# A decoder block's attention: the softmax sums' reciprocals reach all partitions through DRAM instead of through TensorE transposes

## The chip, the cores and the metric

The kernel runs on one core of one Trainium2 chip. The metric is the device time of one execution in microseconds (us), lower is better. The kernel before takes 2318.57 us, the median of three runs (2317.03 to 2318.62). The profile shown here is of one further execution of it.

An engine is one of the core's processors, each with its own in-order instruction stream: PE (TensorE, matrix multiplications), DVE (VectorE), ACT (ScalarE), POOL (GpSimd) and SP (SyncE, which here issues nearly all the DMA transfers). An instruction that waits for another engine or for a transfer holds up everything behind it on its own engine.

## What is computed

The block adds attention and a gated recurrence to a residual stream. The change touches the attention alone:

```
def forgetting_attention(q, k, v, f_logit):
    ...
    def one_block(args):
        qi, ci, bi = args
        qpos = bi * Q_BLOCK + jnp.arange(Q_BLOCK)
        s = jnp.einsum('bhqd,bhkd->bhqk', qi, k, preferred_element_type=jnp.float32) * scale
        s = s + (ci[:, :, :, None] - c[:, :, None, :])
        s = jnp.where(kpos[None, :] <= qpos[:, None], s, -jnp.inf)
        w = jax.nn.softmax(s, axis=-1)
        return jnp.einsum('bhqk,bhkd->bhqd', w.astype(v.dtype), v)
```

There are 8 heads of width 128 and a sequence of 2048 positions. All is float32.

## The kernel before, in words

Every large product is made of three matrix multiplications (`mm3`, lines 60 to 62): an operand is split into a high part, rounded to the format that TensorE takes, and the low rest, and high by high, high by low and low by high are added up in PSUM, the accumulation memory.

The program has three stages. The first (to about 1140 us) makes q, k, v and the gates and runs the recurrence. The second, the attention, follows until about 1740 us. The third mixes the two branches and applies the last gate.

The attention works in **units**: a unit is a head h and a block g of 512 query positions (g from 0 to 3, so 32 units, numbered n). A unit needs keys and values only up to its own end, so block g has 4g+4 key blocks of 128. The schedule is written out by hand in **slots**; each key block of each unit has one slot, and `t0[n]` is the slot at which unit n's probabilities begin to be used. `run_slot(t)` emits, in this order:

- `before[t]`: the loads that were put into this slot (SP)
- the score pieces of a coming unit (`score_units`): `mm3` into a PSUM tile `sbank`, then on DVE (L629) the bias is added, the running row minimum kept in `m` and the result written to `pr`
- `add_values` for the key block of three slots ago (`AHEAD` = 3): `mm3` of values and turned probabilities into `obank`. There is **one** `obank` buffer, so a unit's first `add_values`, in slot t0+3, needs the former unit's result to have been read out
- when that was a unit's last key block, which is in slot t0+2 of the next unit: `finish_unit`, on DVE (L690), `on` = `obank` times `rb`. It reads `obank` out, and the buffer is free
- `turn_probs`: four PE transposes of the probabilities `pr` into a PSUM tile `tbank` (L665), then the split into `th` on ACT (L46) and `tl` on DVE (L52)
- `spread_sums`, in a unit's second slot (t0+1)
- `gate_unit` (L693) and the exponentials of rows that are complete (ACT, L638), which also give the row sums into `r4`
- one slot ahead of t0: the reciprocals of the sums, in place (L842)

The reciprocals stand in `r4` as four columns, one number for each query on its partition. `rb` must hold, on every partition, the 512 numbers along the row. `spread_sums` makes it with four PE transposes of a broadcast column (L684) and an ACT copy out of PSUM (L686):

```
b = psT.tile([P, 512], F32, name="tbank")
for i in range(4):
    nc.tensor.transpose(b[:, i * P:(i + 1) * P], u.r4[:, i:i + 1].broadcast_to([P, P]), ident)
u.rb = av.tile([P, 512], F32, name="rb")
nc.scalar.activation(u.rb, b, AF.Copy)
```

SP issues in this stage the queries `qf`, keys and values `kvf` of the next head, the biases `bias` and `dg`, the gates `gs`, and the stores of `ya_d` (L710), which wait for `gate_unit`. SP is not tied to slots: it runs ahead until an instruction of its queue has to wait. In the last head it also loads the output weights (`kvf` from `in_w_o_dram`), and in the last unit the recurrent branch (`yf`, L716), which ACT and POOL split into `yh` and `yo`; the product of these with the weights is worked off between the last unit's slots (`fill`).

Of the kernel before, what the change touches and what calls it, by code (L numbers as in the profile page):

```python
# [8 lines left out]
F32 = mybir.dt.float32  # L9
# [6 lines left out]
P = 128  # L16
# [49 lines left out]
def hymba_kernel(ctx: ExitStack, tc: tile.TileContext, x, xT, pT, w_t, w_v3, w_v4, w_o, w_ple, w_pg,  # L66
                 w_gates, vecs, rows, mgrp, out):
    nc = tc.nc
# [12 lines left out]
    r_d = dram.tile([NH * 4, 512], F32, name="r_d")  # L81
# [57 lines left out]
    def pool_(stack, name, bufs=1, side="left", space=None):  # L139
        kw = {"side": side} if space is None else {"side": side, "space": space}  # L140
        return stack.enter_context(tc.tile_pool(name=name, bufs=bufs, reuse_waits="tile", **kw))
# [317 lines left out]
    def load_piece(h, n):  # L459
        c = n // 2  # L460
        f = ap.tile([P, 4, P], F32, name="kvf", bufs=3)
        if n % 2 == 0:
            nc.sync.dma_start(out=f.rearrange("p a b -> p (a b)"), in_=kT_d[h, :, c * 512:(c + 1) * 512])
        else:
            nc.sync.dma_start(out=f, in_=v_d[h, :, c * 4:c * 4 + 4])
        pieces[h, n] = f

    def split_piece(h, n):
        if n == 0:
            s = Ctx()  # L470
            kv = kvB if h % 2 else kvA
            s.kh = kv.tile([P, S], F32R, name="kh")
            s.kl = kv.tile([P, S], F32R, name="kl")
            s.vh = kv.tile([P, TB, P], F32R, name="vh")
            s.vl = kv.tile([P, TB, P], F32R, name="vl")
            heads[h] = s
        s = heads[h]
        f = pieces.pop((h, n))
        c = n // 2
        if n % 2 == 0:  # L480
            cs = slice(c * 512, (c + 1) * 512)
            split(nc, f.rearrange("p a b -> p (a b)"), s.kh[:, cs], s.kl[:, cs], "act", "pool")
        else:
            bs = slice(c * 4, c * 4 + 4)
            split(nc, f, s.vh[:, bs], s.vl[:, bs], "act", "pool")
# [119 lines left out]
    av = pool_(p2, "av", 2)  # L605
# [54 lines left out]
    def turn_probs(g, u, sb):  # L660

        q0 = max(0, sb - 4 * g)
        b = psT.tile([P, 512], F32, name="tbank")
        for i in range(q0, 4):
            nc.tensor.transpose(b[:, i * P:(i + 1) * P], u.P[i][:, sb * P:(sb + 1) * P], ident)  # L665
        th = av.tile([P, 512], F32R, name="th", bufs=THB)
        tl = av.tile([P, 512], F32R, name="tl", bufs=THB)
        n = slice(q0 * P, 512)
        split(nc, b[:, n], th[:, n], tl[:, n], "act", "dve")
        u.parts[sb] = (th, tl, n)  # L670

    def add_values(h, g, u, sb):
        s = heads[h]
        nsb = 4 * g + 4
        if sb == 0:
            u.o = psO.tile([P, 512], F32, name="obank")
        th, tl, n = u.parts.pop(sb)
        mm3(nc, u.o[:, n], (s.vh[:, sb], s.vl[:, sb]), (th[:, n], tl[:, n]), sb == 0, sb == nsb - 1)

    def spread_sums(u):  # L680
# [7 lines that stand above are left out]
    def finish_unit(h, g, u):  # L688
        u.on = av.tile([P, 512], F32, name="on")
        nc.vector.tensor_tensor(out=u.on, in0=u.o, in1=u.rb, op=ALU.mult)  # L690

    def gate_unit(u):
        nc.vector.tensor_tensor(out=u.gs, in0=u.on, in1=u.gs, op=ALU.mult)  # L693

    def add_squares(h, g, u):
        on = u.on
        cs = slice(g * 512, (g + 1) * 512)
        eng = nc.vector if (h, g) == (NH - 1, 3) else nc.gpsimd
        if h == 0:
            nc.gpsimd.tensor_tensor(out=acca[:, cs], in0=on, in1=on, op=ALU.mult)  # L700
        else:
            eng.tensor_tensor(out=on, in0=on, in1=on, op=ALU.mult)
            eng.tensor_tensor(out=acca[:, cs], in0=acca[:, cs], in1=on, op=ALU.add)

    def load_gate(h, g, u):
        u.gs = av.tile([P, 512], F32, name="gs")
        nc.sync.dma_start(out=u.gs, in_=gT_d[h, :, g * 512:(g + 1) * 512])

    def store_y(h, g, u):
        nc.sync.dma_start(out=ya_d[h, :, g * 512:(g + 1) * 512], in_=u.gs)  # L710
# [22 lines left out]
    stages = [(h, g) for h in range(NH) for g in range(4)]  # L733
    NS = len(stages)
    t0, t = [], 8
# [4 lines left out]
    units = {0: u0}  # L740
    before = {}
    after = {}

    def at(d, slot, f):
        d.setdefault(max(slot, 0), []).append(f)
# [11 lines left out]
    def begin_unit(n):  # L757
        h, g = stages[n]
        u = units[n]
        u.parts = {}  # L760
        u.units = score_units(h, g, u)
# [16 lines left out]
        at(after, min(lo + 4, s0 - 1) if n > 1 else 0, lambda n=n: mask_u(units[n]))  # L778
    for n, (h, g) in enumerate(stages):
        at(before, max(t0[n] - 4, t0[n - 1] + 7) if n else t0[n] + 1, lambda h=h, g=g, n=n: load_gate(h, g, units[n]))  # L780
    for h in range(1, NH):
        base = t0[4 * (h - 1)]
        for p_ in range(8):
            a = base + (13 if p_ == 0 else 17 + 3 * p_)
            at(before, a - 6, lambda h=h, p_=p_: load_piece(h, p_))
            at(after, a, lambda h=h, p_=p_: split_piece(h, p_))
# [21 lines left out]
    def run_slot(t, fill=None):  # L808
        for f in before.pop(t, ()):
            f()  # L810
        post = []
        for n, j in s_at.pop(t, ()):
            if j == 0:
                begin_unit(n)
            f, a, z = units[n].units[j]
            e = f(a, z)
            if e is not None:
                post.append(e)
        if fill is not None:
            fill()  # L820
        done = None
        if t - AHEAD in slots:
            n, sb = slots[t - AHEAD]
            h, g = stages[n]
            add_values(h, g, units[n], sb)
            if sb == 4 * g + 3:
                done = units.pop(n)
                finish_unit(h, g, done)
                at(after, t + 3, lambda: add_squares(h, g, done))
                at(before, t + 4, lambda: store_y(h, g, done))  # L830
        if t in slots:
            n, sb = slots[t]
            turn_probs(stages[n][1], units[n], sb)
            if sb == 1:
                spread_sums(units[n])
        if done is not None:
            gate_unit(done)
        for e in post:
            e()
        if t + 1 in t0[:NS]:  # L840
            r4 = units[t0.index(t + 1)].r4
            nc.vector.reciprocal(r4, r4)  # L842
        for f in after.pop(t, ()):
            f()

    for t in range(last_t0 + 1):
        run_slot(t)
# [42 lines left out]
    def fill():  # L890
        tb, k = todo.pop(0)
        recurrent_half(tb, (k,))
        if k == KD - 1:
            store_m(tb, av, "th")
            if filling[0]:
                at(before, filling[0] + 1, lambda: load_yf(yl_d, tb + 2))
                at(after, filling[0] + 4, lambda: split_yf(tb + 2))
            else:
                next_y(tb)
# [3 lines left out]
    for t in range(last_t0 + 1, end):  # L903
        filling[0] = t
        run_slot(t, fill if last_t0 + 6 <= t < t0[NS] + AHEAD else None)
    filling[0] = 0
    for t in sorted(set(before) | set(after)):
        run_slot(t)
# [214 lines left out]
```

## Time and profile before

| | us |
|---|---|
| median of three runs | 2318.57 |
| the profiled execution, whole | 2320.89 |
| its span in the trace | 2319.0 |
| of it 0 to 1140 (first stage): PE busy | 1133.00 |
| of it 1140 to 1740 (attention): PE busy | 565.37 |
| of it 1740 to 2319 (third stage): PE busy | 569.72 |

The 1.9 us between the span and the whole execution lie around the program. In rows of the trace a name such as `obank<-th,vh` is the tile written and the tiles read; `x4` counts merged instructions; in the timeline the first number is the start and the second the duration, both in us, and a bracket behind a row is the time that its engine was idle before it, with what came last. PE's matrix multiplications overlap, so on PE the distance between starts is what one costs, not its duration.

### The profile page before, as it was taken

What the parts mean: (1) busy time and instruction counts of PE and PEld (TensorE: products, weight loads), DVE (VectorE), ACT (ScalarE), POOL (GpSimd) and SP (SyncE); (2) the same over time, 40 slices, a digit from 0 to 9 for tenths busy, and PEclk for the clock granted to TensorE, in tenths of its full rate; (3) what the DMA queues carried; (4) which work ended last, traced back from release to release, by engine and by line L of the source; (5) the groups of instructions that cost most, each with busy time, mean ns of one, the idle gap of its engine ahead of it and who ended that gap; (6) DMA issues with size and microseconds to landing.
All of it is one profiled execution on the core that took longest, in us unless ns stands there. A gap on an engine that the chain in (4) does not pass through costs nothing.

```text
span 2319.0 us, 30716 instructions
## 1 busy us (share of the span) xinstructions
PE 2268.1 (98%) x11425; PEld 1887.5 (81%) x11425; DVE 1207.6 (52%) x2190; ACT 926.2 (40%) x1558; POOL 676.7 (29%) x597
## 2 busy tenths in 40 slices
PE   8999999999999999999899999999999999999999
PEld 8998888888888888888777888888877887888887
DVE  5222675454545454646478878788823213333333
ACT  7311433333333232323366666766734323211111
POOL 0120322322323232323033434343444223222221
PEclk9999999999999999999999999999999999999999
DMA  9411112121212121212444454444446435433332
GB/s 337 137 51 37 53 55 71 45 76 37 84 37 84 37 85 37 82 37 78 147 133 130 149 153 143 137 133 128 147 122 199 152 129 191 125 109 118 108 107 77
DMA packets 169013, 249.02 MB, mean 107 GB/s; under 512 B 14240, under 2 KB 87200, under 8 KB 168864
## 3 DMA queue, kind: packets, MB, share of 16 engines
q1 hardware_dynamic: 168720, 247.03, 33.6%
q8 instruction: 89, 1.46, 0.3%
q14 instruction: 60, 0.49, 0.1%
q10 hardware_dynamic: 144, 0.05, 0.0%
HBM read 171.26 MB, written 75.76 MB: 107 GB/s over the span
## 4 chain that ended last, share of the span: by engine, by line
PE 89%; DVE 4%; DMA 2%; ACT 2%; issue 2%; POOL 1%; SPq 1%; DVEq 0%; ACTq 0%; POOLq 0%
PE bank L60 23%; PE bank L62 23%; PE bank L61 23%; PE tbank L665 4%; PE obank L60 2%; PE obank L61 2%; PE obank L62 2%; DVE pr L629 2%; PE sbank L60 2%; PE sbank L61 2%; PE sbank L62 2%; DMA kvf<-in_w_o_dram 1%; PE bank L1023 1%; ACT pr L638 1%; DVE tl L52 1%
## 5 line engine op out<-in xcount | busy, mean ns | idle before, releaser
L60 PE MATMUL bank<-xh,wh 128*128 128x512 f32 x1280 | 506.0, 395 | 0.0
L61 PE MATMUL bank<-xl,wh 128*128 128x512 f32 x1280 | 505.9, 395 | 0.0
L62 PE MATMUL bank<-xh,wl 128*128 128x512 f32 x1280 | 505.9, 395 | 0.0
L61 PEld LDWEIGHTS bank<-xl,wh 128*128 128x128 f32 x1280 | 240.5, 188 | 58.1
L62 PEld LDWEIGHTS bank<-xh,wl 128*128 128x128 f32 x1280 | 240.5, 188 | 58.0
L60 PEld LDWEIGHTS bank<-xh,wh 128*128 128x128 f32 x1280 | 240.5, 188 | 57.7
L52 DVE TENSOR_TENSOR tl<-tbank,th 128x512 fp32r<-128x512 f32 (+1 forms) x320 | 193.4, 608 | 93.4 <-ACT th L46 88.6
L46 ACT ACTIVATE th<-tbank 128x512 fp32r<-128x512 f32 (+1 forms) x320 | 168.5, 529 | 139.9 <-PE tbank L665 133.0
L52 POOL TENSOR_TENSOR wl<-wf,wh 128x512 fp32r<-128x512 f32 x70 | 96.0, 1392 | 265.0 <-ACT wh L46 265.0
L638 ACT ACTIVATE pr<-pr,m 128x128 f32<-128x128 f32 (+15 forms) x128 | 154.0, 1203 | 47.7 <-DVE m L629 47.0
L665 PE MATMUL tbank<-ident,pr 128*128 128x128 f32 x1088 | 172.0, 273 | 0.5 <-DVE tl L52 0.5
L665 PEld LDWEIGHTS tbank<-ident,pr 128*128 128x128 f32 x1088 | 134.1, 140 | 29.7 <-DVE tl L52 0.7
L52 POOL TENSOR_TENSOR yo<-yf,yh 128x1024 fp32r<-128x1024 f32 x32 | 76.8, 2400 | 258.2 <-ACT yh L46 251.8
L60 PE MATMUL bank<-wvh,xh 128*128 128x256 f32 (+1 forms) x512 | 144.2, 286 | 7.0 <-ACT wvh L46 7.0
L60 PE MATMUL obank<-th,vh 128*128 128x512 f32 (+1 forms) x320 | 124.7, 390 | 22.4 <-ACT th L46 11.6
L62 PE MATMUL bank<-wvh,xl 128*128 128x256 f32 (+1 forms) x512 | 144.6, 284 | 0.0
L61 PE MATMUL bank<-wvl,xh 128*128 128x256 f32 (+1 forms) x512 | 144.4, 284 | 0.0
L60 PE MATMUL sbank<-kh,qh 128*128 128x512 f32 (+3 forms) x320 | 134.9, 422 | 7.5 <-DVE m L629 6.5
L61 PE MATMUL obank<-tl,vh 128*128 128x512 f32 (+1 forms) x320 | 117.7, 368 | 1.2 <-DVE tl L52 0.6
L62 PE MATMUL obank<-th,vl 128*128 128x512 f32 (+1 forms) x320 | 117.5, 367 | 0.0
L61 PE MATMUL sbank<-kl,qh 128*128 128x512 f32 (+3 forms) x320 | 116.5, 364 | 0.0
L62 PE MATMUL sbank<-kh,ql 128*128 128x512 f32 (+3 forms) x320 | 116.1, 363 | 0.0
(218 smaller groups left out, 4599.4 us busy)
## 6 DMA issues: line engine op xcount, KB each, us to landing
wf<-in_w_t_dram SPq DMA_DIRECT2D x80, 256.0 KB, 3.0
xr<-in_x_dram SPq DMA_DIRECT2D x16, 512.0 KB, 6.7
v_d<-vo SPq DMA_DIRECT2D x64, 128.0 KB, 2.1
kT_d<-st SPq DMA_DIRECT2D x32, 256.0 KB, 2.1
yl_d<-G SPq DMA_DIRECT2D x32, 256.0 KB, 2.1
qT_d<-st SPq DMA_DIRECT2D x32, 256.0 KB, 2.1
gT_d<-st SPq DMA_DIRECT2D x32, 256.0 KB, 2.1
dg<-nb_d SPq DMA_DIRECT2D x32, 256.0 KB, 7.5
```

Of the source, the lines that this page charges most:

```text
L46: nc.scalar.activation(hi, src, AF.Copy)
L52: eng.tensor_tensor(out=lo, in0=src, in1=f32(hi), op=ALU.subtract)
L60: nc.tensor.matmul(out, lhsT=wh, rhs=xh, start=start, stop=False)
L61: nc.tensor.matmul(out, lhsT=wh, rhs=xl, start=False, stop=False)
L62: nc.tensor.matmul(out, lhsT=wl, rhs=xh, start=False, stop=stop)
L629: nc.vector.tensor_tensor_reduce(out=pr[0][:, a:z], in0=b[:, :z - a], in1=u.dg[i][1] if z == L else u.bias[:, a:z], scale=-1.0, scalar=BIG ...
L638: nc.scalar.activation(pr[0][:, :L], pr[0][:, :L], AF.Exp, bias=m2, scale=-1.0, accum_out=u.r4[:, i:i + 1])
L665: nc.tensor.transpose(b[:, i * P:(i + 1) * P], u.P[i][:, sb * P:(sb + 1) * P], ident)
L1023: nc.tensor.transpose(b[:, k * P:(k + 1) * P], ht[:, kk * P:(kk + 1) * P], ident)
```

## The change

For the units with g > 0 (24 of 32) the reciprocals are no longer turned on TensorE. `store_sums` writes the 128x4 tile to a row of 512 floats in DRAM (`r_d`), in slot t0+1; `load_sums` reads that row back into all 128 partitions, in slot t0+4. Both are issued by SP. The units with g = 0 keep `spread_sums`.

```
+    def store_sums(n):
+        nc.sync.dma_start(out=r_d[n].rearrange("(q p) -> p q", p=P), in_=units[n].r4)
+
+    def load_sums(n):
+        units[n].rb = av.tile([P, 512], F32, name="rb")
+        nc.sync.dma_start(out=units[n].rb, in_=r_d[n:n + 1, :].broadcast_to([P, 512]))
...
+    for n, (h, g) in enumerate(stages):
+        if g > 0:
+            at(before, t0[n] + 1, lambda n=n: store_sums(n))
+            at(before, t0[n] + 4, lambda n=n: load_sums(n))
...
-            if sb == 1:
+            if sb == 1 and stages[n][1] == 0:
                 spread_sums(units[n])
```

`r_d` was declared in the kernel before and not used. In the changed kernel the store of a unit is one transfer of 512 separate numbers of 4 bytes, the load one of 256 KB. The store waits for the reciprocals, the load for the store's landing, and `finish_unit` for the load's landing.

On PE, slot t0+1 of unit (h=3, g=2) before, where `r_11580` is that unit's `r4`:

```order
L665 MATMUL tbank<-ident,pr 128x128 x4
L684 MATMUL tbank<-ident,r_11580 128x128 x4
L60 MATMUL sbank<-kh,qh 128x256
L61 MATMUL sbank<-kl,qh 128x256
L62 MATMUL sbank<-kh,ql 128x256
L60 MATMUL obank<-th,vh 128x128
```

and the same place now:

```order
L665 MATMUL tbank<-ident,pr 128x128 x4
L60 MATMUL sbank<-kh,qh 128x256
L61 MATMUL sbank<-kl,qh 128x256
L62 MATMUL sbank<-kh,ql 128x256
L60 MATMUL obank<-th,vh 128x128
```

Four transposes are gone and nothing else has moved; on ACT the copy of L686 is gone in the same way, and DVE and POOL keep their order.

SP's queue around slot t0+1 of unit (h=3, g=1) before, beginning with the store of the former head's last unit:

```order
L710 DMA ya_d<-gs 128x512
L707 DMA gs<-gT_d 128x512
L463 DMA kvf<-kT_d 128x512
L496 DMA qf<-qT_d 128x512
L710 DMA ya_d<-gs 128x512
L707 DMA gs<-gT_d 128x512
```

and now (the lines of the `ya_d` store and the gate load have become L717 and L714):

```order
L706 DMA r_d<-r_11424 128x4x1
L717 DMA ya_d<-gs 128x512
L714 DMA gs<-gT_d 128x512
L463 DMA kvf<-kT_d 128x512
L710 DMA rb<-r_d 128x512
L496 DMA qf<-qT_d 128x512
L717 DMA ya_d<-gs 128x512
L714 DMA gs<-gT_d 128x512
```

The store of the sums stands ahead of a `ya_d` store, a gate load and a key load, which now come behind its wait; the broadcast load stands ahead of the next queries.

SP's queue at the beginning of the last unit (h=7, g=3) before, where `yf` is the first load of the recurrent branch:

```order
L707 DMA gs<-gT_d 128x512
L591 DMA kvf<-in_w_o_dram 128x512
L716 DMA yf<-yl_d 128x8x128
L591 DMA kvf<-in_w_o_dram 128x512 x4
L716 DMA yf<-yl_d 128x8x128
```

and now:

```order
L714 DMA gs<-gT_d 128x512
L706 DMA r_d<-r_15371 128x4x1
L591 DMA kvf<-in_w_o_dram 128x512
L723 DMA yf<-yl_d 128x8x128
L591 DMA kvf<-in_w_o_dram 128x512 x2
L710 DMA rb<-r_d 128x512
L591 DMA kvf<-in_w_o_dram 128x512 x2
L723 DMA yf<-yl_d 128x8x128
```

Here a weight load and `yf` have come behind the store of the sums, two further weight loads behind the broadcast load.

## The prediction

> **What bounds the kernel now.** I read the page's first part for the busiest engine, then the stretches of the attention stage, then who PE waits for there, and last the timeline around each unit's second slot. The first part gives each engine's busy time and its share of the span:
>
> ```profile
> PE 2268.1 (98%) x11425; PEld 1887.5 (81%) x11425; DVE 1207.6 (52%) x2190; ACT 926.2 (40%) x1558; POOL 676.7 (29%) x597
> ```
>
> The busy times of the attention stage (stretch, its length, then PE, PE's weight loads, DVE, ACT and POOL, PE's granted clock, share of the DMA engines, GB/s):
>
> ```profile
> 1140.00:1740.00 600.00, 565.37 (x3269) 476.73 (x3268) 447.82 (x1091) 393.33 (x720) 233.44 (x258) 0.99 0.46 139
> ```
>
> PE is busy 94% of the stage, DVE 75%, so as a mean PE sets the pace, and work taken off PE should shorten the stage. But a mean over 32 units says nothing of the slots in which the work is taken away. There PE waits, in a few places and again and again. The waits view of PE in this stage (microseconds in all, times, longest):
>
> ```profile
> PE obank L60 <- ACT th L46: 11.6, 15, 0.9
> PE obank L60 <- DVE on L690: 10.7, 16, 1.1
> ```
>
> Both are waits of the first matrix multiplication of an `add_values`. The second kind stands in slot t0+3, two slots behind the one in which the transposes are removed: there is one `obank`, and PE may write the new unit's sums only when `finish_unit` has read the old one's out. So the question is whether that read-out, DVE's `on`, comes earlier when PE does less before it.
>
> **What is removed.** PE's timeline of unit (h=3, g=2): the two rows on top are a slot without `spread_sums`, the three below the slot with it.
>
> ```profile
> 1387.19 0.60 PE L665 MATMUL tbank<-ident,pr 128*128 128x128 f32 x4
> 1387.55 0.48 PE L60 MATMUL sbank<-kh,qh 128*128 128x512 f32 x1
> ...
> 1388.68 0.60 PE L665 MATMUL tbank<-ident,pr 128*128 128x128 f32 x4
> 1389.12 0.60 PE L684 MATMUL tbank<-ident,r 128*128 128x128 f32 x4
> 1389.47 0.36 PE L60 MATMUL sbank<-kh,qh 128*128 128x256 f32 x1
> ```
>
> From the first L665 to the scores 0.36 us pass without the four transposes, and 0.79 us with them: they cost PE 0.43 us. In 24 units that is 10.3 us, if PE gets on with it. Now the same 24 units at slot t0+3.
>
> For **g=2**, `on` (one row of the mask before it, then the accumulator read) and PE's first use of `obank` after it:
>
> ```profile
> 1390.62 0.48 DVE L629 CUSTOM_DVE_ANT_0 pr<-sbank,dg,m 128x256 f32<-128x256 f32 x1
> 1391.02 0.08 DVE L629 DVE_READ_ACCUMULATOR2_ANT m<- 128x1 f32 x1
> 1391.02 0.69 DVE L690 TENSOR_TENSOR on<-obank,rb 128x512 f32<-128x512 f32 x1
> ...
> 1392.07 0.39 PE L60 MATMUL obank<-th,vh 128*128 128x512 f32 x1
> ```
>
> `on` ends at 1391.71. DVE stands behind other DVE work there without a gap, so it comes no earlier. PE takes up a result of DVE about 0.14 us after its end (the next two places show it), so it could go on at 1391.85 and does at 1392.07. Of the 0.43 us saved, 0.22 bring something forward; the rest becomes a wait that isn't there now.
>
> For **g=3**, (h=3, g=3), the chain that leads to `on`:
>
> ```profile
> 1409.61 0.60 ACT L46 ACTIVATE th<-tbank 128x512 fp32r<-128x512 f32 x1 [0.55 <-PE tbank L665]
> ...
> 1410.24 0.69 DVE L52 TENSOR_TENSOR tl<-tbank,th 128x512 fp32r<-128x512 f32 x1
> ...
> 1410.85 0.68 DVE L690 TENSOR_TENSOR on<-obank,rb 128x512 f32<-128x512 f32 x1
> ...
> 1411.68 0.47 PE L60 MATMUL obank<-th,vh 128*128 128x512 f32 x1 [0.92 <-ACT th L46]
> ```
>
> `th` starts when the L665 transposes of slot t0+1 are done, which stand **ahead** of L684; `tl` follows `th`, `on` follows `tl`. Nothing on this path has to do with the removed instructions. `on` ends at 1411.53, PE starts 0.15 later and has already waited 0.92 us. It will wait 1.35. Gain: nothing.
>
> For **g=1**, (h=3, g=1), DVE has no idle time at all ahead of `on`:
>
> ```profile
> 1375.23 0.69 DVE L52 TENSOR_TENSOR tl<-tbank,th 128x512 fp32r<-128x512 f32 x1
> ...
> 1375.83 0.61 DVE L629 CUSTOM_DVE_ANT_0 pr<-sbank,dg,m 128x384 f32<-128x384 f32 x1
> 1376.37 0.09 DVE L629 DVE_READ_ACCUMULATOR2_ANT m<- 128x1 f32 x1
> 1376.37 0.69 DVE L690 TENSOR_TENSOR on<-obank,rb 128x512 f32<-128x512 f32 x1
> ...
> 1377.20 0.47 PE L60 MATMUL obank<-th,vh 128*128 128x512 f32 x1 [0.47 <-DVE on L690]
> ```
>
> DVE sets the pace here, `on` ends at 1377.06, PE comes 0.14 later after 0.47 us of waiting, which become 0.90. Gain: nothing.
>
> The removed ACT copy stands behind the `th` that matters in each of the three places, and `on` reads the former unit's `rb`, so it isn't on the path either. **Sum: 8 x 0.22 = 1.8 us**, out of 10.3.
>
> **What is added.** DVE's `on` now waits for a transfer, and SP for two things: the store for the reciprocals, the load for the store. Who is queued behind: at g=1 the `ya_d` store, a gate load and a key load, then the next queries; behind them only things that are needed much later. The tightest case for `on` is g=1, with the reciprocal, and SP's rows of before around it:
>
> ```profile
> 1369.88 0.32 SPq L710 DMA_DIRECT2D ya_d<-gs  x1
> ...
> 1372.59 0.17 DVE L842 RECIPROCAL r<-r 128x4 f32<-128x4 f32 x1
> ...
> 1374.56 0.32 SPq L707 DMA_DIRECT2D gs<-gT_d  x1
> ```
>
> The store can go at 1372.8 and pushes the `ya_d` store from 1369.88 to 1373.2. The gate load waits for that one's landing (4.7 us before), so it issues at about 1377.9, the key load behind it, the load of `rb` at about 1378.7. Landing times from the list of DMA issues (median, last number):
>
> ```profile
> dg<-nb_d SPq DMA_DIRECT2D x32, 256.0 KB, 7.5
> ...
> qf<-qT_d SPq DMA_DIRECT2D x30, 256.0 KB, 4.2
> ...
> nb_d<-nb SPq DMA_DIRECT2D x4, 64.0 KB, 1.7
> ```
>
> A load of the same 256 KB lands 4.2 to 7.5 us later, at 1382.9 to 1386.2. `on` of this unit is the row at 1391.02 above: 4.8 to 8.1 us to spare. g=2 and g=3 have longer, since their units have more slots. For the store there is no row with pieces of 4 bytes. The `nb_d` store, 128 pieces, lands in 1.7 us; this one has 512 pieces, so 6.8 us if all of the time went by pieces. I take 2, nearest to the row; at 6.8 it would land at 1379.6, the load at 1387.1 at worst, still ahead of `on`. Cost on PE from both sides: nothing.
>
> The Trainium skill, "DMA: Bandwidth & Descriptors", Specifications, says that below 512 bytes a transfer does a read-modify-write; it gives no price for it, and no run here shows one. By it the store could be slower than my upper bound, which is the last rival below.
>
> In the last unit, `yf` comes behind the store. Its issue, the reciprocal that the store now waits for, and its use:
>
> ```profile
> 1680.45 0.44 SPq L716 DMA_DIRECT2D yf<-yl_d  x1
> ...
> 1684.51 0.17 DVE L842 RECIPROCAL r<-r 128x4 f32<-128x4 f32 x1
> ...
> 1691.46 1.05 ACT L46 ACTIVATE yh<-yf 128x1024 fp32r<-128x1024 f32 x1
> ```
>
> SP issues the store at 1684.7, a weight load, and `yf` at about 1685.4. The list of DMA issues has for it:
>
> ```profile
> yf<-yl_d SPq DMA_DIRECT2D x16, 512.0 KB, 4.2
> ```
>
> It lands at 1689.6, 1.9 us before ACT wants it. That cover of 6.8 us shrinks to 1.9; if it were gone, PE, which waits for this split, would pay each further microsecond once. I take nothing, with 1 us as the far end.
>
> So 1.8 us come off the profiled execution's 2320.89, which gives 2319.1. That execution is 2.3 us above the median of the runs, so from the median 2318.57: **2316.8 us**.
>
> **Rivals.**
>
> *PE is the bound, and all of it counts.* 10.3 us less, 2308.3. For it: PE's 94%. Against it: at 16 of the 24 places PE is already waiting in slot t0+3. It would need `on` to move up with PE. The Trainium skill, "Perfetto Trace Analysis", Identifying the Most-Contended Engine, holds the engine with the highest occupancy to be the one to relieve first; by that rule this rival would be the forecast. The trace has PE as the busiest, 94%, and the waits at these slots against it.
>
> *The profile's chain is right about g=3.* The chain that ended last runs there through the removed copy and the next `th`:
>
> ```profile
> 1410.21 0.49 ACT rb L686
> ...
> 1411.18 0.49 ACT th L46
> 1411.68 0.47 PE obank L60
> ```
>
> Then PE waits for ACT, `th` comes 0.49 earlier, and 0.43 is gained in each of 8 units: 3.4 more, 5.2 in all, 2313.4. Against it: the `th` in question ends hardly before PE starts, while `on` ends 0.15 before, the same distance as at g=1, where no other engine is in question; and the multiplication reads a `th` made three slots earlier. I hold the wait for one on DVE under a wrong name.
>
> *The store is slow, and `on` waits for `rb`.* This is the way to a slower kernel. It decides from a landing of 10.7 us on (1372.8 plus that, plus 7.5, is 1391.0); above it, DVE, and PE through `obank`, pay each microsecond in each of the 8 units with g=1. At 12.7 us: 2 x 8 = 16 us, less the 1.8, about 2333. For it: 512 pieces of 4 bytes, which no row shows, and SP's queue held for as long. Against it: it is six times the nearest row.
>
> That the transposes would not go, or come back elsewhere, I leave out: the order of instructions shows PE shorter by them and otherwise the same.
>
> **Chances.** Absorbed, 2316.8 (its own range 2314.5 to 2319): 0.70. All counts, 2308.3: 0.10. The chain is right, 2313.4: 0.08. Late `rb` or loads behind it: 0.12, from about 2319 up. About 0.2% (4.6 us) is what a measurement of this kernel can tell from no change. Faster by more than that: the second case and half of the third, 0.14. Slower by more: nearly all of the fourth, 0.11. Within it: 0.75. The range reaches from 2311, which takes in the chain's case, to 2324, which takes in the lower end of a late `rb`; the second case and most of the fourth are left out, about 0.2.
>
> **What would show it.** In the profile after, the L684 group has 32 instructions and PE's busy time falls by about 10, while PE's idle time in the attention grows by about 8.5: the wait of `obank` for `on` becomes some 0.9 us at g=1, 1.35 at g=3, and about 0.2 at g=2, where there was none. DVE has no wait for `rb`. If instead PE's waits stay as they are, the second case holds; if `on` waits for a DMA, the last; if the waits at g=3 vanish, the chain's. I would be wrong above all if `on` moves up with PE, or if SP, held by the store, delivers the next head's biases or keys too late.

## The result, and the profile after

| | before | after |
|---|---|---|
| median, us | 2318.6 (2317.03 to 2319.09, 4 runs) | 2406.27 (2405.04 to 2409.96, 4 runs) |
| span of the profiled execution, us | 2319.0 | 2404.3 |

The ratio is 1.0379, 95% interval 1.0367 to 1.0391: the change costs 88 us, and 2406 lies far outside the predicted range. The page's first part for the kernel after:

```profile
PE 2288.0 (95%) x11329; PEld 1897.6 (79%) x11329; DVE 1196.3 (50%) x2190; ACT 915.2 (38%) x1534; POOL 676.6 (28%) x597
```

PE has 96 instructions fewer than before and is busy 20 us **longer**. To see where, take the stretch from the first unit's reciprocal to the last unit's `on`, first of before, then of after (columns as in the prediction; the last but two is PE's granted clock):

```profile
1155.60:1728.10 572.50, 544.51 (x3182) 460.24 (x3181) 439.05 (x1068) 384.25 (x702) 228.51 (x252) 1.00 0.46 137
```

```profile
1154.40:1816.70 662.30, 567.76 (x3085) 473.34 (x3084) 428.90 (x1067) 372.97 (x678) 227.62 (x252) 0.93 0.48 129
```

The stretch grew by 89.8 us, so all of the loss is here; the rest of the program is 4.5 us shorter than in this execution of before. PE's idle time grew from 28.0 to 94.5 us (+66.5), and its busy time by 23.3, at a mean granted clock of 0.93. The waits view of PE over this stage names what it idles for:

```profile
PE obank L60 <- DVE on L690: 38.4, 24, 4.2
PE sbank L60 <- DVE m L629: 38.0, 12, 6.7
PE bank L60 <- ACT yh L46: 11.1, 1, 11.1
```

The same view of SP and of ACT:

```profile
SPq L714 <- DMA ya_d<-gs: 178.3, 30, 12.1
SPq L710 <- DMA r_d<-r: 158.6, 17, 11.8
...
ACT kh L46 <- DMA kvf<-kT_d: 62.0, 14, 8.7
ACT vh L46 <- DMA kvf<-v_d: 17.8, 11, 2.3
```

SP now stands 158.6 us waiting for the store's landing (L710 is the load that needs it), and ACT 62.0 us for key loads, of which the same view of before has no row. DVE's waits have no row in which `on` waits for a DMA. From the list of DMA issues (last number: median us to landing):

```profile
kvf<-v_d SPq DMA_DIRECT2D x28, 256.0 KB, 8.4
rb<-r_d SPq DMA_DIRECT2D x24, 256.0 KB, 4.5
...
r_d<-r SPq DMA_DIRECT2D x24, 2.0 KB, 10.5
```

The store of 2 KB takes longer to land than the loads of 256 KB; the trace's view of its line gives 8.6, 10.5 and 13.6 us as least, median and most (the trace tells the landing of 22 of the 24 stores).

Which units pay is read from the reciprocals, one for each unit. Here are those of (h=3, g=3) and of the next unit, in before and in after:

```profile
1407.95 0.17 DVE L842 RECIPROCAL r<-r 128x4 f32<-128x4 f32 x1
...
1432.78 0.17 DVE L842 RECIPROCAL r<-r 128x4 f32<-128x4 f32 x1
```

```profile
1439.48 0.17 DVE L853 RECIPROCAL r<-r 128x4 f32<-128x4 f32 x1
...
1474.48 0.17 DVE L853 RECIPROCAL r<-r 128x4 f32<-128x4 f32 x1
```

This unit took 24.8 us before and takes 35.0. The same difference of neighbouring reciprocals, summed for each g over the heads (the last unit to the end of its `on`), for the kernels that matter below:

| us | g=0 | g=1 | g=2 | g=3 (7 units) | last unit |
|---|---|---|---|---|---|
| before | 71.8 | 107.2 | 175.7 | 174.2 | 43.5 |
| after | 71.7 | 108.4 | 184.0 | 244.9 | 53.3 |
| no transfers (e1) | 72.2 | 107.3 | 174.0 | 174.2 | 43.5 |
| store alone (e2) | 71.3 | 107.3 | 176.6 | 174.2 | 52.8 |
| load that doesn't wait (e3) | 72.6 | 107.9 | 184.5 | 180.1 | 52.6 |
| load later (e6) | 71.5 | 107.3 | 177.3 | 187.2 | 53.0 |

The loss is 70.7 us at g=3, some 10 in each of seven units, then 9.8 in the last unit and 8.3 at g=2. More than half of the 8.3 is one unit, (h=7, g=2), which takes 26.3 us in place of 21.8: ACT waits 4.0 us there for an output weight, and PE 4.2 us behind it. What happens in a unit with g=3 is seen in SP's timeline of after, (h=3, g=3), from the store on:

```profile
1444.43 0.42 SPq L706 DMA_DIRECT2D r_d<-r  x1
1444.97 0.44 SPq L465 DMA_DIRECT2D kvf<-v_d  x1
1454.52 0.32 SPq L710 DMA_DIRECT2D rb<-r_d  x1
1454.88 1.73 SPq L502 DMA_DIRECT2D bias<-nb_d  x1
1456.65 1.85 SPq L508 DMA_DIRECT2D dg<-nb_d  x4
1458.55 0.44 SPq L463 DMA_DIRECT2D kvf<-kT_d  x1
```

and in ACT's, DVE's and PE's rows a little later:

```profile
1465.68 0.63 ACT L46 ACTIVATE kh<-kvf 128x512 fp32r<-128x512 f32 x1 [6.19 <-DMA kvf<-kT_d]
...
1466.83 0.69 DVE L52 TENSOR_TENSOR tl<-tbank,th 128x512 fp32r<-128x512 f32 x1 [6.61 <-ACT th L46]
...
1462.74 0.40 PE L60 MATMUL obank<-th,vh 128*128 128x512 f32 x1
1462.98 0.39 PE L61 MATMUL obank<-tl,vh 128*128 128x512 f32 x1
...
1468.05 0.79 PE L60 MATMUL sbank<-kh,qh 128*128 128x512 f32 x1 [4.23 <-DVE m L629]
...
1470.46 0.63 PE L60 MATMUL obank<-th,vh 128*128 128x512 f32 x1
1470.88 0.63 PE L61 MATMUL obank<-tl,vh 128*128 128x512 f32 x1
```

For 9.5 us, from 1444.97 to 1454.52, SP issues nothing: its next instruction is the load of `rb`, which needs the landed store. Behind it stand the biases and the next head's keys. The keys' load goes at 1458.55, 19.1 us after the reciprocal; in before it went 5.6 us after it:

```profile
1413.58 0.32 SPq L463 DMA_DIRECT2D kvf<-kT_d  x1
```

Not all of these 13.5 us are this one stand. SP had stood once before, 10.9 us for the `rb` of the unit with g=2:

```profile
1426.14 0.50 SPq L465 DMA_DIRECT2D kvf<-v_d  x1
1437.01 0.32 SPq L710 DMA_DIRECT2D rb<-r_d  x1
```

After that it issues the next queries 4.5 us behind the reciprocal (1443.96), where in before it was 0.2 us (1408.11). So two stands add up at g=3.

ACT reaches the split of these keys, waits 6.19 us, and does not do the `th` behind it, which itself needs no transfer; then `tl` is late, the masked scores behind `tl`, and PE. After the gap PE is also slower: from L60 to L61 of the same product (128x512, into `obank`) it is 0.24 us ahead of the gap and 0.42 after it, and the granted clock is 0.50 from 1466.5 to 1473.1. The whole unit by windows:

```profile
1444.00:1475.00 31.00, 25.24 (x123) 21.07 (x124) 16.61 (x39) 15.03 (x32) 11.91 (x14) 0.83 0.60 170
```

As a mean the granted clock is 0.83 in this stretch of after; in before it is 1.00 from the first reciprocal to the last `on` (above). The Trainium skill, "TensorE: Matmul & The Clock Gate", Part 1, says that after an idle window of about 3.4 us the array's clock falls back to half rate; the trace agrees as far as the gap of 4.23 us is followed by products 1.75 times as long, but in e4 (below) a gap of 1.73 us was enough.

### The profile page after: what moved, and what is told of

The parts are those of the page before. It is cut to its first block, busy times and chain, and to the rows that moved or that the text cites. A ratio compares the mean times of both kernels' runs of the same rounds, so it can differ in the third digit from the quotient of the medians.

```text
span 2404.3 us, 30553 instructions
## 1 busy us (share of the span) xinstructions
PE 2288.0 (95%) x11329; PEld 1897.6 (79%) x11329; DVE 1196.3 (50%) x2190; ACT 915.2 (38%) x1534; POOL 676.6 (28%) x597
## 4 chain that ended last, share of the span: by engine, by line
PE 77%; DMA 14%; DVE 3%; ACT 2%; issue 2%; SPq 1%; POOL 1%; DVEq 0%; ACTq 0%; POOLq 0%
PE bank L60 23%; PE bank L62 23%; PE bank L61 23%; DMA r_d<-r 4%; DMA ya_d<-gs 2%; DMA dg<-nb_d 2%; DVE pr L629 2%; PE tbank L665 2%; DMA kvf<-kT_d 2%; DMA qf<-qT_d 1%; PE obank L60 1%; DMA kvf<-in_w_o_dram 1%; PE obank L61 1%; PE obank L62 1%; PE sbank L60 1%
## 5 line engine op out<-in xcount | busy, mean ns | idle before, releaser
L60 PE MATMUL bank<-xh,wh 128*128 128x512 f32 x1280 | 506.0, 395 | 0.0
L61 PE MATMUL bank<-xl,wh 128*128 128x512 f32 x1280 | 505.9, 395 | 0.0
L61 PEld LDWEIGHTS bank<-xl,wh 128*128 128x128 f32 x1280 | 240.5, 188 | 58.1
L60 PEld LDWEIGHTS bank<-xh,wh 128*128 128x128 f32 x1280 | 240.5, 188 | 57.8
L665 PE MATMUL tbank<-ident,pr 128*128 128x128 f32 x1088 | 179.0, 282 | 0.5 <-DVE tl L52 0.5
L60 PE MATMUL obank<-th,vh 128*128 128x512 f32 (+1 forms) x320 | 131.3, 410 | 48.7 <-DVE on L690 38.4
L60 PE MATMUL sbank<-kh,qh 128*128 128x512 f32 (+3 forms) x320 | 140.1, 438 | 39.0 <-DVE m L629 38.0
L665 PEld LDWEIGHTS tbank<-ident,pr 128*128 128x128 f32 x1088 | 140.1, 146 | 31.8 <-issue 2.2
L60 PE MATMUL bank<-wvh,xh 128*128 128x256 f32 (+1 forms) x512 | 143.9, 285 | 7.0 <-ACT wvh L46 7.0
L61 PE MATMUL bank<-wvl,xh 128*128 128x256 f32 (+1 forms) x512 | 143.9, 283 | 0.0
L61 PE MATMUL obank<-tl,vh 128*128 128x512 f32 (+1 forms) x320 | 123.1, 385 | 1.1 <-DVE tl L52 0.6
L61 PE MATMUL sbank<-kl,qh 128*128 128x512 f32 (+3 forms) x320 | 120.0, 375 | 0.0
```

The costliest lines, as they stand in the source:

```text
L60: nc.tensor.matmul(out, lhsT=wh, rhs=xh, start=start, stop=False)
L61: nc.tensor.matmul(out, lhsT=wh, rhs=xl, start=False, stop=False)
```

## The experiments

All times are medians in us; the ratio is to the kernel before, run on the same chip, with its 95% interval.

| run | us | ratio |
|---|---|---|
| e1, no transfers | 2317.44 | 0.9992 [0.9984, 1.0001] |
| e2, store alone | 2331.00 | 1.0057 [1.0043, 1.0071] |
| e3, load that doesn't wait | 2343.26 | 1.0110 [1.0096, 1.0124] |
| e4, 16-byte pieces | 2330.33 | 1.0053 [1.0037, 1.0069] |
| e5, last unit as before | 2383.40 | 1.0278 [1.0264, 1.0292] |
| e6, load later | 2343.40 | 1.0106 [1.0091, 1.0122] |
| e7, 16-byte pieces, put in order by POOL | 2315.57 | 0.9982 [0.9973, 0.9991] |
| e8, e1 with two obanks | 2308.04 | 0.9953 [0.9941, 0.9966] |
| e9, before with two obanks | 2331.95 | 1.0058 [1.0044, 1.0071] |
| e10, e7 with two obanks | 2305.66 | 0.9944 [0.9931, 0.9956] |
| e11, half the store | 2328.91 | 1.0037 [1.0024, 1.0050] |
| e12, store issued by POOL | 2317.58 | 0.9992 [0.9983, 1.0001] |
| e13, pieces 512 bytes apart | 2320.24 | 1.0004 [0.9994, 1.0014] |
| e14, both transfers issued by POOL | 2340.54 | 1.0094 [1.0073, 1.0114] |
| e15, e14 with two obanks | 2321.49 | 1.0013 [1.0003, 1.0023] |
| e16, the change again | 2397.55 | 1.0340 [1.0325, 1.0356] |
| e17, pieces 64 bytes apart | 2320.84 | 1.0003 [0.9992, 1.0014] |

One of e9's five executions took 4526.42 us, and nothing on record says why; the ratio leaves it out, and the median of the other four is 2331.8.

**The removal by itself (e1).** The edit to the change:

```
+        if g == 0:
+            head_rb[h] = u.rb
-        nc.vector.tensor_tensor(out=u.on, in0=u.o, in1=u.rb, op=ALU.mult)
+        nc.vector.tensor_tensor(out=u.on, in0=u.o, in1=head_rb[h], op=ALU.mult)
...
-            at(before, t0[n] + 1, lambda n=n: store_sums(n))
-            at(before, t0[n] + 4, lambda n=n: load_sums(n))
```

> The removal alone: blocks g > 0 take the reciprocals of their head's first block (so the values of 24 units are scaled by other sums), and there is no store and no load. If the saving is absorbed by the one obank, as forecast: 1 to 3 us less than before, 2316 to 2318, with PE's wait for DVE's on growing by about 8 us. If all of the removed PE work counts: 10 us less, 2308. If the removal itself costs time (PE's order, the clock): a good part of the 88 us stays, above 2330.

1.6 us less than before, which can't be told from no change. PE's waits for `obank` in e1:

```profile
PE obank L60 <- DVE on L694: 25.0, 24, 1.4
...
PE obank L60 <- ACT th L46: 4.3, 8, 0.8
```

Together 29.3 us, where before had 22.3: most of what PE saves it waits for `on`. So the missing 88 us are all on the transfers' side.

**Store, load, and SP's wait between them (e2, e3, e6).** e2 keeps the transposes and adds the store; e3 loads a row that landed long ago (the block of the former head), so that the load has nothing to wait for; e6 is the change with the load later, in slot t0+6, 9 or 12.

```
e2  -            at(before, t0[n] + 4, lambda n=n: load_sums(n))
    ...
    -            if sb == 1 and stages[n][1] == 0:
    +            if sb == 1:
e3  +        row = r_d[n - 4:n - 3, :] if n >= 4 else nb_d[0, 0:1, :512]
    -        nc.sync.dma_start(out=units[n].rb, in_=r_d[n:n + 1, :].broadcast_to([P, 512]))
    +        nc.sync.dma_start(out=units[n].rb, in_=row.broadcast_to([P, 512]))
e6  -            at(before, t0[n] + 4, lambda n=n: load_sums(n))
    +            at(before, t0[n] + 3 + 3 * g, lambda n=n: load_sums(n))
```

> The store of the sums as in the change, but no load: every unit makes rb with the transposes as before. SP never waits for the store's landing here, though it still waits for the reciprocals. Theory A, SP held up by its wait for the store's landing is the cost: within 5 us of before, 2318 to 2323. Theory B, the store itself, with its 512 pieces, blocks the DMA rings that all later transfers stand behind for some 10 us: most of the 88 us stays, 2360 to 2400.

> Store and load as in the change, but the load reads the row that the same block of the former head stored (for the first head a row of biases), so it has no store in flight to wait for; the values of 24 units are scaled by other sums. Theory A, SP's wait for the landing: the 88 us go, 2316 to 2325. Theory B, the store blocks the rings: 2370 to 2406, with the landings of the transfers right behind a store still at 10 us.

> The change, with the load of the sums moved from slot t0+4 to slot t0+6 (g=1), t0+9 (g=2) and t0+12 (g=3), so that SP issues the other loads first and comes to the wait when the store has landed or nearly so. Theory A (SP's wait for the landing at g=3 is the bulk of it): the g=3 units come back from some 35 us to 25 or 26 each, and the time is 2325 to 2345, with the 9 us of the last unit and the key and value loads behind the store left over. If the bulk is the traffic or the clock and not the place of the wait: 2380 to 2406.

The table of the units shows it. The store alone costs nothing at g=3 and 9.2 us in the last unit. With transfers that don't wait for each other (e3), g=3 loses 5.9 us in place of 70.7, and the whole 24 in place of 88: **SP's wait for the landing is 63 us of the 88** (54, if taken from e16). A load issued late enough (e6) gives nearly the same time by another way: in e6 the wait of the load for the store is down from 158.6 us to one of 6.9.

```profile
SPq L717 <- DMA r_d<-r: 24.2, 6, 5.1
...
SPq L710 <- DMA r_d<-r: 6.9, 1, 6.9
```

The 24.2 us at L717, a store of `ya_d` put down to the same landing, are new. e6 loses 13.0 us at g=3, and there the load comes too late for its own consumer. DVE's waits in e6 have a row that after doesn't have:

```profile
DVE on L690 <- DMA rb<-r_d: 6.2, 5, 2.9
```

Three of the seven units lose 11.4 of the 13.0 us. In each of them `on` waits for `rb`, the former unit's (0.8, 2.9 and 2.0 us), PE waits for `on`, and the unit's granted clock is 0.94, 0.89 and 0.94.

What is left in e3, and in the last unit of e6, are transfers that land late behind a store. Worked out from every transfer's issue and landing: in e2, between 1150 and 1700 us, SP issued 50 others while a store was under way, as far as the trace tells the landings (18 of the 24 stores), and none landed before that store, the earliest 0.2 us after it; they took 10.2 us in the median, against 4.8 for the rest. In the last unit the weight loads and `yf` are among them, and PE's wait for `yh` there is 9.5 us in e2, 11.1 in after. ACT splits them in order, and in after it stands 7.9 and 2.1 us at two weight loads (`Wh`) and not at `yf`, whose split stands behind them.

**The last unit (e5, and e16).** e5 is the change with the last unit's transposes kept; e16 is the change itself, in another set of runs (the record doesn't name the chip of the first).

```
-        if g > 0:
+        if g > 0 and n < NS - 1:
...
-            if sb == 1 and stages[n][1] == 0:
+            if sb == 1 and (stages[n][1] == 0 or n == NS - 1):
```

> The change as it is, but the last unit keeps its transposes, so that its store is not ahead of the first yf load on SP's queue. Theory (the last unit's 9.7 us are the yf load landing behind the store): 2396 to 2398. Rival (the time is lost at the end to something else, such as the clock or the loads of the output's weights): 2403 to 2407.

> The change as it is, once more. The form whose last unit keeps its transposes gave 2383 where 2396 to 2398 was expected, though its instructions up to the last unit are those of the change; its stores landed in 9.8 us against 10.5. If the landing differs from chip to chip: 2390 to 2400 here, with a landing near 9.8. If not: 2404 to 2410 and a landing near 10.5, and the last unit's store would have cost 23 us in some way that is not seen yet.

The last unit falls from 53.3 to 43.2 us in e5, the expected 10, so the loss there comes from the store ahead of the weight loads and `yf`; PE's wait for `yh` there goes from 11.1 to 1.0. But e5 came out 13 us below the expected range, for reasons outside that unit. e16 explains most of it: the same change took 2397.55 in that set, with a landing of 9.5 us against 10.5, while the medians of the kernel before in all these sets lie within 1.1 us. Against e16, e5 is 14 us faster, where its last unit accounts for 11.3 (54.5 us in e16); the two were on different chips. By the same sums as in the table, the remaining 3 us are 5.5 less at g=2 and 2.3 more at g=3; their cause stays open.

**Why the landing is long (e4, e11, e13, e17).** e4 is the change with the row in another order, so that the store has 128 pieces of 16 bytes in place of 512 of 4; `on` then reads `rb` with a stride. The others are e2 with another store: two of the four columns, and all pieces apart in DRAM (e = 128 or 16 floats; `r_d` is that much longer).

```
e4   +        nc.sync.dma_start(out=r_d[n].rearrange("(p q) -> p q", p=P), in_=units[n].r4)
     ...
     +            nc.vector.tensor_tensor(out=u.on.rearrange("c (q p) -> c q p", p=P),
     +                                    in0=u.o.rearrange("c (q p) -> c q p", p=P),
     +                                    in1=u.rb.rearrange("c (p q) -> c q p", p=P), op=ALU.mult)
e11  +        nc.sync.dma_start(out=r_d[n, 0:256].rearrange("(q p) -> p q", p=P), in_=units[n].r4[:, 0:2])
e13  +        nc.sync.dma_start(out=r_d[n].rearrange("(q p e) -> p q e", p=P, e=P)[:, :, 0], in_=units[n].r4)
e17  +        nc.sync.dma_start(out=r_d[n].rearrange("(q p e) -> p q e", p=P, e=16)[:, :, 0], in_=units[n].r4)
```

> The same numbers through DRAM in another order: each partition stores its four reciprocals as one piece of 16 bytes, so 128 pieces and not 512, and DVE reads rb with a stride. If the store's landing goes by the number of pieces (10.5 us now, 32 pieces for each of 16 DMA engines, some 0.3 us a piece): it lands after 3.5 to 4.5 us and the time is 2316 to 2330. If it goes by the bytes or is one fixed delay of short writes: it lands after 10 us as now, and the time stays at 2395 to 2410.

> The form that only stores, with the first two of the four columns: 256 pieces of 4 bytes, 16 for each DMA engine. Landing by number of pieces (3.1 us at 128 pieces, 9.9 at 512): about 5 to 6 us, and the time about 2324 to 2327, since the last unit's yf lands half as late. Landing by the instruction, whatever its pieces: 9 to 10.5 us and 2329 to 2333.

> The form that only stores, its 512 pieces of 4 bytes now 512 bytes apart in DRAM, so that no two of them lie in the same 512 bytes; number and size of the pieces, queue and slots stay. Pieces that share a stretch of DRAM wait for each other (so 128 pieces of 16 bytes landed in 3.1 us, and 256 pieces of 4 bytes still took 8.9): a landing of 2 to 5 us and 2318 to 2324. The piece of 4 bytes itself is slow, wherever it lies: 9 to 11 us and 2328 to 2333.

> The form that only stores, its 512 pieces of 4 bytes 64 bytes apart. With 512 bytes between them they landed in 3.6 us, side by side in 9 to 10. If the stretch for which neighbouring pieces wait is 64 bytes or less: 3 to 4.5 us and 2317 to 2322. If it is longer (such as 512 bytes, eight pieces each): between 4.5 and 10 us.

The store's row in the lists of DMA issues of e4, e11, e13 and e17, in this order:

```profile
r_d<-r SPq DMA_DIRECT2D x24, 2.0 KB, 3.1
```

```profile
r_d<-r SPq DMA_DIRECT2D x24, 1.0 KB, 8.9
```

```profile
r_d<-r SPq DMA_DIRECT2D x24, 2.0 KB, 3.6
```

```profile
r_d<-r SPq DMA_DIRECT2D x24, 2.0 KB, 3.5
```

After e4 I held that the landing goes by the number of pieces; e11 took that away (256 pieces, 8.9 us where 5 to 6 were expected). For pieces of 4 bytes, what decides is whether they lie **side by side**: the same 512 pieces land in 3.5 us when 64 bytes apart, and e13 and e17 cost nothing that can be measured. Lying side by side isn't slow by itself: the 16-byte pieces of e4 do so too and land in 3.1 us. Whether the size of a piece counts, or how many share 64 bytes (16 of 4 bytes, 4 of 16), no run takes apart. The Trainium skill, "DMA: Bandwidth & Descriptors", Specifications, which the prediction weighed, has a read-modify-write for every transfer below 512 bytes; here that alone is not what is slow, since pieces of 4 bytes land in 3.5 us where no two share 64 bytes. e4 still lost 11 us, in part because the strided read makes DVE's `on` longer:

```profile
L693 DVE TENSOR_TENSOR on<-obank,rb 128x512 f32<-128x512 f32 x24 | 25.6, 1068 | 1.4 <-PE obank L62 1.4
```

It takes 1.07 us in place of 0.69. A unit's `on` runs in the next unit's third slot, so the longer ones fall into units with g=2, g=3 and g=0. By the sums of the table, e4 loses 3.0 us against e1 at g=2, which is 8 x 0.38, and 5.9 at g=3, where 7 x 0.38 is 2.7, nothing at g=0, and 2.0 in the last unit. DVE has idle time in this stage, so these are one more sign that `on` sets the pace at g=2 and g=3. Most of the other 3.2 us at g=3 is the clock: in two units PE waits 1.73 us for `on` and is then granted half its clock. In one of them (columns as in the prediction):

```profile
1271.20:1274.60 3.40, 1.67 (x13) 1.28 (x12) 3.30 (x7) 2.16 (x5) 0.99 (x1) 1.00 0.79 208
1274.70:1278.00 3.30, 3.30 (x14) 2.90 (x13) 1.44 (x2) 0.83 (x2) 0.20 (x1) 0.50 0.78 214
```

So a gap half as long as the one named above is enough at times. The same wait in the other units didn't do it; what decides, the traces don't show.

**Another queue (e12, e14, e15).** e12 is e2 with the store issued by POOL; e14 is e6 with both transfers issued by POOL; e15 is e14 with two obanks (`PS = 422`).

```
e12, e14  -        nc.sync.dma_start(out=r_d[n].rearrange("(q p) -> p q", p=P), in_=units[n].r4)
          +        nc.gpsimd.dma_start(out=r_d[n].rearrange("(q p) -> p q", p=P), in_=units[n].r4)
e14       +        nc.gpsimd.dma_start(out=units[n].rb, in_=r_d[n:n + 1, :].broadcast_to([P, 512]))
```

> The form that only stores, its stores issued by POOL in place of SP. If what is issued behind a store lands late because it stands in the same queue: ya_d's stores land in about 3.5 us and the kvf loads of v_d in 4 as before the change, yf isn't late, and the time is 2318 to 2322 (a few us more if POOL's own work waits behind the store's wait for DVE's r). If the small pieces hold the DMA engines themselves, whichever queue they come from: 6 to 8 us for both, yf late by some 9 us, 2328 to 2333.

> The change with its stores and loads issued by POOL in place of SP, the loads three slots later for each block of the head; values and pieces as in the change. If the loss is that SP waits for the store's landing and that SP's own loads queue behind the store: 2315 to 2322. If the store's 4-byte pieces slow everything in flight whoever issues them, or POOL's copies of keys and values come late behind its wait for the landing: 2330 to 2345.

> The same with two obanks and two tbanks. If POOL's queue hides the transfers: 2303 to 2310, as the form of 16-byte pieces gave 2305.7 with one unit's transposes more. If POOL's wait for the landing delays its copies: 2315 to 2340.

e12 costs nothing, but not for the reason that I had in mind. Its transfers still land late:

```profile
ya_d<-gs SPq DMA_DIRECT2D x32, 256.0 KB, 6.2
kvf<-kT_d SPq DMA_DIRECT2D x28, 256.0 KB, 7.9
kvf<-v_d SPq DMA_DIRECT2D x28, 256.0 KB, 6.2
```

against 3.5, 6.4 and 4.0 in before, though not strictly behind the store any more (some land up to 5.1 us ahead of it). What went is the last unit's loss: SP doesn't wait for the reciprocal, and issues a weight load at 1677.81 and `yf` at 1678.19, ahead of POOL's store at 1683.21. That is a change of order, so e12 doesn't tell a queue's order from a shared resource. e14 lost 21.5 us, 17.5 of them at g=3. POOL now stands before the stores, until the reciprocals are there:

```profile
POOL r_d L706 <- DVE m L629: 66.5, 8, 8.4
```

Its loads of `rb` come late with it, and as in e6 `on` waits for them:

```profile
DVE on L690 <- DMA rb<-r_d: 8.6, 9, 1.7
```

At g=3 six of seven units take 27.4 to 28.0 us, against 24.8 to 25.2 in before; in each of the six `on` waits 0.6 to 1.7 us for `rb`, and the granted clock is 0.94. e15, with two obanks, is level with before; there too `on` waits for `rb`, 14.6 us in 9 waits.

**What the transposes cost with another bank (e8, e9).** e8 is e1 with `PS = 422`, e9 is the kernel before with it: two obanks and two tbanks in place of one and three.

> The removal alone again (reciprocals of the head's first block, no transfers), with two obank buffers and two tbank buffers in place of one and three. If the one obank is what absorbs the saving, this is 6 to 10 us faster than the kernel before with the same two obanks. If something else absorbs it, 1 to 3 us.

> The kernel before with two obank and two tbank buffers: the reference for the run above. The 18 us that PE waits for DVE's on should go; what two tbanks cost in place of three is not known, so 2300 to 2330.

The transposes are worth 1.6 us with one obank and **23.9 us** with two. In e9 PE has no wait for `obank`; it waits for `tbank`, of which `spread_sums` takes one of two:

```profile
PE tbank L665 <- DVE tl L52: 16.3, 29, 1.5
PE tbank L684 <- DVE tl L52: 7.6, 21, 0.6
PE tbank L665 <- ACT rb L686: 5.2, 16, 0.4
```

```profile
PE tbank L665 <- DVE tl L52: 15.9, 23, 1.5
...
PE tbank L684 <- DVE tl L52: 4.8, 8, 1.3
```

(e9 above, e8 below.) From the first reciprocal to the last, by windows of e9 and of e8:

```profile
1155.50:1700.10 544.60, 515.22 (x2982) 428.92 (x2981) 431.42 (x1046) 370.05 (x672) 208.95 (x239) 1.00 0.46 137
```

```profile
1154.50:1673.90 519.40, 496.56 (x2890) 415.99 (x2889) 422.33 (x1047) 356.46 (x649) 211.39 (x240) 1.00 0.48 144
```

18.7 us less busy time of PE and 6.5 less idling. I had expected less than half: with two tbanks the transposes hold a buffer that the next slot wants, which they hardly do with three (PE's waits for `tbank` in before are 0.5 us). The runs change both numbers of buffers at once, so what the second obank adds by itself isn't shown, nor why the busy time falls by more than the 10.3 us of the prediction.

**A version that beats both (e7, e10).** 16-byte pieces, the load later, the last unit's transposes kept, and POOL puts the row in order, so that `on` reads it without a stride; e10 adds `PS = 422`.

```
+    def order_sums(n):
+        u = units[n]
+        u.on = av.tile([P, 512], F32, name="on")
+        nc.gpsimd.tensor_copy(u.on.rearrange("c (q p) -> c q p", p=P), u.rb.rearrange("c (p q) -> c q p", p=P))
+        u.rb = u.on
...
+            at(before, t0[n] + 3 + 2 * g, lambda n=n: load_sums(n))
+            at(after, t0[n] + 4 + 3 * g, lambda n=n: order_sums(n))
```

> All that the runs so far show put together: pieces of 16 bytes (landing about 3 us), the load in slots t0+5, t0+7 and t0+9, the order of the numbers put right by a POOL copy off DVE's path, and the last unit left with the transposes. If the causes found are all of it: 2316 to 2321, no more than the 1.8 us of the removal faster than before. If a fixed cost of the detour is left: 2325 to 2335.

> The form of 16-byte pieces (128 pieces a store, a later load, a copy on POOL that puts the order right, transposes kept in a head's first block and in the last unit), now with two obanks and two tbanks. Theory (the removal is worth much where the transposes take one of two tbanks, and the store costs nothing once it lands in about 3.4 us and SP does not wait for it): 2306 to 2311, as the form without transfers with two obanks gave 2308.0 and this one keeps one unit's transposes. Rival (POOL's copies or the loads come late for the earlier order that two obanks allow): 2315 to 2335, with PE's obank waiting for DVE's on, and on for POOL.

e7 is 3.6 us below before, about what e1 gains (1.6; the intervals overlap). e10 takes 2305.66, 14 us less than before. Its page has PE at

```profile
PE 2257.5 (98%) x11333; PEld 1874.1 (81%) x11333; DVE 1205.5 (52%) x2190; ACT 916.0 (40%) x1535; POOL 702.1 (30%) x620
```

10.6 us less than before, and POOL's 23 copies add 25.

## Why the prediction was wrong

**What bounds the kernel: right.** `on` through the single `obank` sets the pace, not PE's 94%. e1 shows it (what is saved ahead of `on` is waited for at `obank`), and e4 at g=2 and g=3 (a longer `on` is paid for). The pair e8 and e9 agrees, though it changes two buffers at once.

**What is removed: right, and the size in part by luck.** 1.8 us were forecast, 0.22 in each unit with g=2. The table has 1.7 for e1 at g=2 and nothing at g=1 and g=3; but five units gain 0.26 to 0.31, one 0.16 and two hardly anything, and the median, 1.6 below, isn't clear of noise. The waits for `obank` grew by 7.0 where 8.5 were forecast, and PE's busy time from the first reciprocal to the last `on` fell by 7.4, not 10. The rival by which all of it counts falls, and with it the one that read the chain at g=3 as it stands: the copy is gone, and g=3 is as long as before.

**What is added: this step failed, in two places.** The first is the size of one term: the store's landing was "I take 2", with 6.8 as the upper bound if all of the time went by pieces; it is 8.6 at the least and 10.5 in the median. The bound was worked out from 128 pieces of `nb_d`, which don't lie side by side in this way. The sentence on the Trainium skill's rule said that the store could be slower than the bound; the sum didn't use it.

The second is "behind them only things that are needed much later". That was read at g=1, the tightest place for `on`, and holds there (g=1 lost 1.2 us in eight units, 1.1 of it in the last head). At g=3 the next head's biases and keys stand behind the load of `rb`. In before the keys issued at 1413.58 landed in 7.4 us and were split by ACT at 1423.95, so they had 3.0 us to spare; a stand of SP of 9.5 us is far beyond that, and the stand for the unit before it comes on top. The last paragraph named this ("if SP, held by the store, delivers the next head's biases or keys too late") and the last case had "loads behind it", but no time was worked out for it.

**The last unit: mis-sized.** "I take nothing, with 1 us as the far end", where `yf` was forecast to land 1.9 us ahead of its use. The cover of 1.9 us was worked out from a landing of 4.2 us as in before; behind the store, the weight load ahead of `yf` took 12.6 us (1764.06 to 1776.68), and `yh` waits behind its split: 9.8 us, once.

**The rival of the slow store had the cause and not the path.** Its point of decision, 10.7 us, is nearly the landing measured, but `on` never waits for `rb` in the change: the load of `rb` landed in 4.5 us in the median, and not 7.5. Only where the load was moved back (e6, e14, e15) did that path appear. The rival priced 16 us at g=1; the loss is 70.7 at g=3, over SP, the keys, ACT, DVE and PE. Of the 89.8 us, 23.3 are not idling but products at a lower clock, although the removal takes 7.4 off PE's busy time (e1).

## What to carry to other kernels

A transfer's cost isn't its landing beside its own consumer, but everything that its queue holds behind the wait: look for the next deadline behind it in **every** kind of unit, not at the tightest place of the transfer itself. Where a removed piece of work stands ahead of a wait for a single buffer, count what the wait takes back, and see which buffer it used: the same removal was worth 1.6 us with one obank and three tbanks, and 23.9 with two of each. A load that is moved back to spare its queue can come too late for its own consumer (e6, e14). A term that no row shows and that sits at the head of a queue deserves a price for its bad case, above all when the bound is drawn from a store of another form.

## What was not expected of the hardware

- A store of 512 pieces of 4 bytes that lie side by side in DRAM lands in 8.6 to 13.6 us in after (median 10.5); 64 or 512 bytes apart in 3.5 and 3.6 in the median; 128 pieces of 16 bytes side by side in 3.1. Why neighbours of 4 bytes are slow, the traces don't show. The median of the same store differed between two sets of runs of the change, 10.5 and 9.5, and the kernel by 9 us, while the kernel before agreed within 1.1 us; whether the chip is the cause isn't shown.
- What SP issued while a store was under way landed after it in each of the 50 cases of e2 whose landing the trace tells, 0.2 us at the earliest. The Trainium skill, "DMA: Bandwidth & Descriptors", Queues, rings and completion order, says that a completion is counted only after every earlier write of the same DMA engine; the 50 cases agree. It says so across queues too; in e12, with the store in POOL's queue, 7 of 116 landed up to 5.1 us before it, so that no run here settles that part.
- DVE's product with one operand read at a stride of 16 bytes takes 1.07 us in place of 0.69 (128x512).
- A wait of PE of 1.73 us was followed by 3.4 us at a granted clock of 0.50 (in two units of e4, not in the others); in after, 6.8 us at that clock begin within the gap of 4.23 us.
